# A fifth raw weight tile, the output projection's B21 split before its T4, and the context gate's tiles taken from the raw ring

## The chip, the core and the metric

The kernel runs as one program on one core of a Trainium2 chip. The metric is the device time of one execution in microseconds (us). Three runs of the kernel before took 925.86, 922.6 and 922.02 us, median 922.6.

## The reference, cut to what matters

One layer of a token mixer with a gated feed-forward network, on 512 tokens of width 1024 in float32, with 256 context tokens whose scan states start the scans of the main tokens. The parts that the change touches:

```python
la = jax.nn.log_sigmoid(lr @ w2 + b2) / 16      # gate of each head, for tokens and for context
o, s_f, s_b = _gla_bidir(q, k, v, lr, w2, b2, s0f, s0b)   # 4 heads, both directions, s0 from the context
...
merged = sigmoid(ga) * (a @ w_br_a) + sigmoid(gb) * (ob @ w_br_b)
x = x + g1 * (merged @ w_o)                     # the output projection
h2 = rms_norm(x) * (1 + scale) + shift
a, val = split(h2 @ w_up)                       # ffn, then a 3x3 convolution, gelu, and w_down
```

The last lines stand in a shortened form. The modulations (g1, scale, shift) are dot products of silu(c) with w_ada.

## The kernel before, in words

Every large product runs on TensorE with float32 operands taken apart into a high and a low half: the high half (wh, a cast) is made on ScalarE, the low half (wl, the weight minus its high half) on VectorE, and each product is three matmuls, high x high, high x low and low x high. So each weight tile costs ScalarE one 128x1024 cast (L149) and VectorE one 128x1024 subtraction (L150), both in `split_new`.

Weights arrive as raw tiles. They come from one ring, the tag `raw`, with four tiles; the load of a fifth weight waits until the first tile has been split. The high and low halves have rings of their own, with five tiles each. The list `specs` holds the splits in the order in which products use them, and `loads` what has to be loaded ahead of each; `weights` hands out the next split, makes the splits up to a lead (`stream_split`), and issues loads further ahead (`stream_load`). As every engine and the load queue on SyncE (SP) work strictly in program order, the place at which these calls stand in the code decides what waits behind what.

The square projections use a Strassen scheme of seven products on 512x512 blocks: `strassen` runs the products, `w_strassen` lists the weight splits. For the output projection (w_o, `low_first`) the products come in the order a11, s3, s2, s1, a22, a12, s4, each in two halves j. Their weights are B11, T3, T2, B12, T4, B21 and B22. T2 and T4 are sums of blocks, made in the tiles tt (L223 casts and L224 subtractions in `split_t`, sums at L236 and by accumulating loads of GpSimd). Between s2 and s1 the sum so far is copied from one pair of PSUM banks to another, on ScalarE (L483), and another sum is added into the first pair on VectorE (L484). `wo_done` takes each finished bank: `wo_gate` multiplies it with g1 (L1511, tile yt), `wo_add` adds it to the residual (L1515, tile x), `wo_sq` sums squares (L1518). The products of s4 end in the last pair of banks, for tokens 0 and 1 and the second half of the columns. Once these two yt are made, `low_norm` turns the second norm's outputs around for the ffn: transposes on TensorE (L1495), high and low halves h2h and h2l (L1503, L1504, L1506, L1507). The xs of the norm are scaled on ScalarE (L1487). The first ffn products are L402.

`wo_step` counts the 14 product halves; at the last of them it makes four more splits of ffn weights at once, so that these stand in the engines' queues ahead of the last yt.

The gate of the context tokens (`zc_head`, `zc_tail`, once per head) reads one PSUM bank (zc) into two tiles of the general ring `heap`: lc by ScalarE (L851), mc by VectorE (L853), then Exp, Ln, two scans on VectorE (L863), Exp (L865), and the product with the context's keys (L931), before TensorE transposes it (L949). `zx_head` and `zx_tail` do the same for the main tokens, with four short scans for each direction (L902). The rings also set order: a tile or a bank that is not yet free holds up what writes it.

In the opening, `cs` holds silu(c) for both modulations, in 32 columns for each of 8 blocks, cleared first (L527); the later modulations `ada2` read one column of it (L1190). `ones` is a constant 128x128 tile, and `ones_r` a rounded copy of it.

Of the kernel before, what the change touches and what calls it, by code (L numbers as in the profile page):

```python
# [8 lines left out]
F32 = mybir.dt.float32  # L9
F32R = mybir.dt.float32r  # L10
# [3 lines left out]
ALU = mybir.AluOpType  # L14
AX = mybir.AxisListType

P = 128
# [16 lines left out]
def backbone_kernel(  # L34
# [19 lines left out]
    def nm(s):  # L54
        cnt[0] += 1
        return f"{s}_{cnt[0]}"
# [16 lines left out]
    def const(shape, s, dt=F32):  # L73
        return cp.tile(shape, dt, tag=s, name=s)
# [23 lines left out]
    def table_for(func):  # L98
# [4 lines left out]

    ident = const([P, P], "ident")
    make_identity(nc, ident)
    ones = const([P, P], "ones")
    G.memset(ones, 1.0)
    maskf = const([P, P], "maskf")
    G.affine_select(out=maskf, in_=ones, pattern=[[1, P]], base=0, channel_multiplier=-1,
                    compare_op=ALU.is_ge, fill=0.0)  # L110
    maskb = const([P, P], "maskb")
    G.affine_select(out=maskb, in_=ones, pattern=[[-1, P]], base=0, channel_multiplier=1,
                    compare_op=ALU.is_ge, fill=0.0)
    eps_t = const([P, 1], "eps_t")
    G.memset(eps_t, EPS)
# [25 lines left out]
    specs, loads, last_load = [], [], {}  # L141

    def raw_tile(kn, n):
        return wp.tile([P, kn, n], F32, tag="raw", name=nm("raw"), bufs=4)

    def split_new(raw, kn, n):
        wh = wp.tile([P, kn, n], F32R, tag="wh", name=nm("wh"))
        wl = wp.tile([P, kn, n], F32R, tag="wl", name=nm("wl"))
        A.copy(wh, raw)  # L149
        V.tensor_tensor(wl, raw, wh.bitcast(F32), op=ALU.subtract)  # L150
        return wh, wl

    def w_cols(w, c0, n=P, k0=0, kn=KT, scaled=False):
        ap = w[k0 * P:(k0 + kn) * P, c0:c0 + n].rearrange("(k p) c -> p k c", p=P)
# [28 lines left out]
    def w_strassen(w, c0, add_b12=False, low_first=False):  # L183
# [58 lines left out]
        def split_b11(j):  # L242
            def split():
# [4 lines left out]
        js = range(2)  # L248
        b21, t1 = [split_raw("b21", j) for j in js], [split_raw("b12", j) for j in js]
        t4 = [lambda j=j: split_t(j) for j in js]  # L250
        specs.extend([split_b11(j) for j in js] + [(lambda j=j: split_t(j)) for j in js] + [split_t2(j) for j in js] +
                     (t1 + t4 + b21 if low_first else b21 + t1 + t4) + [split_raw("b22", j) for j in js])
        for o, fs in ((0, [load_raw("b11", 0, 0, j) for j in js]), (2, [load_t(j) for j in js]),
# [43 lines left out]
    def weights(lead=1, ahead=AHEAD):  # L297
# [9 lines left out]
    NG = len(GROUPS)  # L307
    G0 = [sum(GROUPS[:i]) for i in range(NG)]
    fv = [tuple(wp.tile([P, 2, 512], dt, tag=tag, name=nm(tag), **kw)
                for tag, dt, kw in (("raw", F32, dict(bufs=4)), ("wh", F32R, {}), ("wl", F32R, {})))  # L310
          for _ in range(4)]
    fqk = []
    w_lr = late([P, KT, 32], s="w_lr")
# [209 lines left out]
    A.activation(sg, cT, AF.Exp, scale=-1.0)  # L523
    V.tensor_scalar(sg, sg, 1.0, None, op0=ALU.add)
    V.reciprocal(sg, sg)
    cs = const([P, KT, 32], "cs")
    V.memset(cs, 0.0)  # L527
    V.tensor_tensor(cs[:, :, 0], cT[:, 0:8], sg[:, 0:8], op=ALU.mult)
    V.tensor_tensor(cs[:, :, 1], cT[:, 8:16], sg[:, 8:16], op=ALU.mult)

    selm = const([P, 4], "selm")
    for i in range(4):
# [308 lines left out]
    def zc_head(h):  # L841
        S_ = heads[h]
        bcol, wz = gate_col(h)
        zc = gl()
        for d in range(2):
            T.matmul(zc[:, d * LC:(d + 1) * LC], wz[d], lrc, start=True, stop=True)

        l = heap([P, 2, LC], s="lc")
        m = heap([P, 2, LC], s="mc")
        for d in range(2):  # L850
            A.activation(l[:, d, :], zc[:, d * LC:(d + 1) * LC], AF.Abs, bias=bcol[d])  # L851
        for d in range(2):
            V.tensor_scalar(m[:, d, :], zc[:, d * LC:(d + 1) * LC], bcol[d], 0.0, op0=ALU.add, op1=ALU.min)  # L853
        S_["zc"] = l, m
# [322 lines left out]
    def ada2(kinds):  # L1177
# [8 lines left out]
        for k in range(KT):  # L1186
            for a_, (_, _, c0) in zip(acc, todo_):
                w_ = late([P, 512], s="wa2")
                dma(w_, w_ada[0, k * P:(k + 1) * P, c0:c0 + 512])
                V.scalar_tensor_tensor(a_, w_, cs[:, k, 0:1], a_, op0=ALU.mult, op1=ALU.add)  # L1190
                yield
        parts = []
        for a_ in acc:
# [29 lines left out]
        V.tensor_copy(ccol[:, i * 110:(i + 1) * 110], ps[:, :110])  # L1223

    bg.extend([ada2(("g1", "sh")), ada2(("sc",))])
    ones_r = const([P, P], "ones_r", F32R)
    V.tensor_copy(ones_r, ones)


    a_act = []  # L1230

# [285 lines left out]
    def wo_sq(hf, t, tmp):  # L1517
        A.activation(tmp, x1[t][hf], AF.Square, accum_out=ss2[:, t, hf:hf + 1])  # L1518

    tmps = {}  # L1520

    def wo_done(hf, t, src, sign):
        if hf and t < 2:
            tmps[hf, t] = wo_gate(hf, t, src)
            if t == 1:
                low_norm()
            return
        tmp = wo_gate(hf, t, src)
        wo_add(hf, t, tmp, sign)
        if t < 2:  # L1530
            tmps[hf, t] = tmp
            return
        wo_sq(hf, t, tmp)
        if hf == 0:
            norm2_xs((t,), (norm2_root(t),))
            if t == 3:
                order_from.append(len(traced()))
# [20 lines left out]
    def wo_step():  # L1558
        count[0] += 1
        if count[0] == 1:  # L1560
            x1_load()
            table_for(AF.Sqrt)
        if count[0] == 14:
            stream_split(pos[2] + 4)
        do()

    strassen(lambda name, k, t: [z[:, k * P:(k + 1) * P] for z in mg[name, t]], wo_done, wo_step, True)
# [69 lines left out]
    def d_raw(kind, p):  # L1637
        if kind == "b22":
            t_ = heap([P, 512], s="b22")
            dma(t_, tokens(2 * p + 1)[:, 512:])  # L1640
            G.dma_start(t_, tokens(2 * p)[:, 512:], accum_op=ALU.add)  # L1641
        else:
            t_ = wp.tile([P, 2, 512], F32, tag="raw", name=nm("raw"), bufs=4)
            dma(t_, tokens(2 * p + (kind == "rb")).rearrange("p (a c) -> p a c", c=512))
        dq[kind, p] = t_

# [289 lines left out]
```

## Time and profile before

| | us |
|---|---|
| median of three runs | 922.6 |
| the profiled execution | 921.73 |
| its span, from the first to the last instruction | 919.7 |
| TensorE busy | 899.5 |
| VectorE busy | 755.4 |
| ScalarE busy | 484.7 |
| mean granted TensorE clock | 0.995 of full |

PE is TensorE, DVE VectorE, ACT ScalarE, POOL GpSimd and SP the engine that issues most loads. The span is cut into 40 slices of 23 us; in all but the first and the last of them, and one in the middle, TensorE is busy for 90% and more. Matmuls overlap: one counts as busy from its start to its end, although the next starts before that end, so short gaps don't show in the busy time. They show in the view of waits and in the starts of the single matmuls. In a row of the timeline stand the start, the duration, the engine, the line, the operation, the tile written and those read, the shapes and the count; in brackets stand the idle time before it and what ended it.

### The profile page before, as it was taken

The numbers are of one execution on the slowest core, as the hardware profiler recorded it, in microseconds if no ns is written. First come the engines' busy times: TensorE is split into PE (matmuls) and PEld (weight loads), VectorE is DVE, ScalarE is ACT, GpSimd is POOL, SyncE is SP. The second block draws the span as 40 slices with busy tenths as digits, with TensorE's granted clock in tenths as the row PEclk, the third lists the DMA queues.
The fourth block names the chain that finished last, engine by engine and source line by source line (L and its number), as shares of the span: only waits on it lengthen the run. The fifth ranks groups of instructions, "written<-read, shape, count | busy, mean of one in ns | idle before, by whom it ended". The sixth has DMA issues, their size and how long they took to land.

```text
span 919.7 us, 12868 instructions
## 1 busy us (share of the span) xinstructions
PE 899.5 (98%) x4671; PEld 756.4 (82%) x4671; DVE 755.4 (82%) x1307; ACT 484.7 (53%) x869; POOL 62.8 (7%) x98
## 2 busy tenths in 40 slices
PE   7999999999999999999999998999999999999996
PEld 5777899988888888888888888988888888888885
DVE  5667686779589877978776887899998888899896
ACT  5156464657466447566552568543333443356673
POOL 3000000000000011113011010000000000122100
PEclk9999999999999999999999999999999999999998
DMA  9950512142088375978578164264444333399532
GB/s 275 338 159 1 154 31 59 34 115 70 15 279 306 97 202 124 288 171 219 160 206 206 33 175 138 69 178 131 126 131 133 104 91 115 79 231 260 151 92 92
DMA packets 125821, 134.27 MB, mean 146 GB/s; under 512 B 7178, under 2 KB 84310, under 8 KB 125758
## 3 DMA queue, kind: packets, MB, share of 16 engines
q1 hardware_dynamic: 115357, 116.80, 41.0%
q0 software_dynamic: 8672, 15.43, 10.3%
q10 hardware_dynamic: 1728, 1.22, 0.4%
q8 instruction: 37, 0.61, 0.3%
q14 instruction: 27, 0.21, 0.1%
HBM read 131.32 MB, written 2.10 MB: 145 GB/s over the span
## 4 chain that ended last, share of the span: by engine, by line
PE 89%; DVE 6%; ACT 2%; issue 1%; DMA 1%; ACTq 0%; DVEq 0%
PE mm L387 31%; PE mm L418 11%; PE gl L465 7%; PE gl L1719 6%; PE mm L465 5%; PE mm L1719 4%; PE gl L418 4%; PE gl L935 3%; PE mm L402 3%; PE mm L708 2%; PE mm L411 2%; PE gl L708 1%; PE mm L1041 1%; DVE mx L902 1%; PE gl L631 1%
## 5 line engine op out<-in xcount | busy, mean ns | idle before, releaser
L149 ACT CAST wh<-raw 128x1024 fp32r<-128x1024 f32 x110 | 115.0, 1050 | 113.4 <-PE mm L387 73.1
L150 DVE TENSOR_TENSOR wl<-raw,wh 128x1024 fp32r<-128x1024 f32 x110 | 133.6, 1220 | 34.2 <-ACT wh L149 31.7
L1602 DVE SCALAR_TENSOR_TENSOR cacc<-ca,ccol,cacc 128x441 f32<-128x441 f32 (+2 forms) x176 | 121.0, 693 | 6.7 <-ACT cacc L1590 3.6
L387 PE MATMUL mm<-h2l,wh 128*128 128x512 f32 x320 | 124.5, 389 | 0.0
L387 PE MATMUL mm<-h2h,wl 128*128 128x512 f32 x320 | 124.5, 389 | 0.0
L387 PE MATMUL mm<-h2h,wh 128*128 128x512 f32 x320 | 124.5, 389 | 0.0
L387 PEld LDWEIGHTS mm<-h2h,wl 128*128 128x128 f32 x320 | 60.1, 188 | 12.6
L387 PEld LDWEIGHTS mm<-h2l,wh 128*128 128x128 f32 x320 | 60.1, 188 | 12.5
L387 PEld LDWEIGHTS mm<-h2h,wh 128*128 128x128 f32 x320 | 60.1, 188 | 12.4
L1190 DVE SCALAR_TENSOR_TENSOR acc<-wa,cs,acc 128x512 f32<-128x512 f32 x64 | 45.8, 747 | 3.4 <-DMA wa<-in_w_ada_dram 3.4
L1605 ACT ACTIVATE cacc<-cacc 128x512 f32<-128x512 f32 x22 | 13.9, 632 | 60.6 <-DVE cacc L1602 60.5
L387 PE MATMUL mm<-hxh,wh 128*128 128x512 f32 x104 | 41.7, 401 | 0.0
L387 PE MATMUL mm<-hxh,wl 128*128 128x512 f32 x104 | 40.9, 394 | 0.0
L387 PE MATMUL mm<-hxl,wh 128*128 128x512 f32 x104 | 40.5, 390 | 0.0
L223 ACT CAST wh<-tt 128x512 fp32r<-128x512 f32 x48 | 28.3, 621 | 20.4 <-DMA tt<-in_w_in_dram 7.5
L224 DVE TENSOR_TENSOR wl<-tt,wh 128x512 fp32r<-128x512 f32 x48 | 31.6, 687 | 7.9 <-ACT wh L223 7.8
L1661 ACT CAST wh<-raw 128x1024 fp32r<-128x1024 f32 x22 | 23.0, 1052 | 18.2 <-PE mm L1719 9.0
L199 POOL DMA_DIRECT2D tt<-in_w_in_dram x24 | 20.8, 1064 | 165.5 <-DVE xl L1291 71.8
L1662 DVE TENSOR_TENSOR wl<-raw,wh 128x1024 fp32r<-128x1024 f32 x22 | 26.9, 1223 | 2.6 <-ACT wh L1661 2.6
L1641 POOL DMA_DIRECT2D b<-in_ffn_w_down_dram x11 | 9.4, 865 | 276.8 <-DMA b<-in_ffn_w_down_dram 268.3
L465 PE MATMUL mm<-wh,hxh 128*128 128x512 f32 x72 | 28.0, 389 | 0.0
L465 PE MATMUL mm<-wl,hxh 128*128 128x512 f32 x72 | 28.0, 389 | 0.0
(527 smaller groups left out, 2449.9 us busy)
## 6 DMA issues: line engine op xcount, KB each, us to landing
raw<-in_w_in_dram SPq DMA_DIRECT2D x54, 512.0 KB, 4.6
wa<-in_w_ada_dram SPq DMA_DIRECT2D x96, 256.0 KB, 5.0
raw<-in_ffn_w_up_dram SPq DMA_DIRECT2D x44, 512.0 KB, 3.9
raw<-in_ffn_w_down_dram SPq DMA_DIRECT2D x22, 512.0 KB, 3.3
tt<-in_w_in_dram POOLq DMA_DIRECT2D x24, 256.0 KB, 6.5
raw<-in_w_br_a_dram SPq DMA_DIRECT2D x8, 512.0 KB, 5.2
raw<-in_w_br_b_dram SPq DMA_DIRECT2D x8, 512.0 KB, 3.8
raw<-in_w_o_dram SPq DMA_DIRECT2D x8, 512.0 KB, 6.0
```

The costliest lines, as they stand in the source:

```text
L149: A.copy(wh, raw)
L150: V.tensor_tensor(wl, raw, wh.bitcast(F32), op=ALU.subtract)
L223: A.copy(wh[:, kk, :], tt[j][kk])
L224: V.tensor_tensor(wl[:, kk, :], tt[j][kk], wh[:, kk, :].bitcast(F32), op=ALU.subtract)
L387: T.matmul(ps, a[:, k, :], b[:, c0:c0 + n], start=(k == 0 and i == 0), stop=(k == KT - 1 and i == 2))
L402: T.matmul(pss[u], a[:, k, :], b[:, c0:c0 + n], start=(k == 0 and z == 0), stop=(k == KT - 1 and z == 2))
L418: T.matmul(ps, a, b[:, k % 2, :], start=(k == 0 and i == 0), stop=(k == KT - 1 and i == 2))
L465: T.matmul(ps[t], a, b[:, kk, :], start=(first and i == 0), stop=(j == 1 and kk == 1 and i == 2), skip_group_check=again)
L708: T.matmul(fps[i], a, b, start=(k == 0 and z == 0), stop=(k == KT - 1 and z == 2))
L1190: V.scalar_tensor_tensor(a_, w_, cs[:, k, 0:1], a_, op0=ALU.mult, op1=ALU.add)
L1602: V.scalar_tensor_tensor(o, a_[:, r0 + dy:r1 + dy, c0 + dx:c1 + dx], wcol(tap), o, op0=ALU.mult, op1=ALU.add)
L1719: T.matmul(ps, a[:, t * P:(t + 1) * P], w[b][:, j, c0:c0 + n], start=(first and i == 0), stop=(last and i == 2), skip_group_check=again)
```

## The change

Five edits go together:

- The ring `raw` has five tiles instead of four.
- Room: `ones` is now `ones_r` read as plain float32, its first copy a short-lived tile; `cs` is a tile of `heap`, cleared where it is used, and its one column that is read later is kept in a small constant `c_col`.
- The context gate's two tiles lc and mc are the two halves of one raw tile, `lm`.
- In the output projection the split of half j of T4 is preceded by the load and the split of half j of B21; the products keep their order and take B21 from `kept`.
- At the last product half the low half of the fourth ffn weight is put off until the last two yt have been made.

```diff
-        return wp.tile([P, kn, n], F32, tag="raw", name=nm("raw"), bufs=4)
+        return wp.tile([P, kn, n], F32, tag="raw", name=nm("raw"), bufs=5)
...
         A.copy(wh, raw)
-        V.tensor_tensor(wl, raw, wh.bitcast(F32), op=ALU.subtract)
+        low = lambda: V.tensor_tensor(wl, raw, wh.bitcast(F32), op=ALU.subtract)
+        if low_later:
+            low_later[0].append(low)
+        else:
+            low()
         return wh, wl
...
         t4 = [lambda j=j: split_t(j) for j in js]
+        if low_first:
+            kept = {}
+
+            def split_both(j):
+                stream_load(base + 11 + j)
+                kept[j] = split_raw("b21", j)()
+                return split_t(j)
+
+            t4 = [lambda j=j: split_both(j) for j in js]
+            b21 = [lambda j=j: kept.pop(j) for j in js]
...
-    cs = const([P, KT, 32], "cs")
+    cs = heap([P, KT, 32], s="cs")
     V.memset(cs, 0.0)
...
+    c_col = const([P, KT], "c_col")
+    V.tensor_copy(c_col, cs[:, :, 0])
...
-        l = heap([P, 2, LC], s="lc")
-        m = heap([P, 2, LC], s="mc")
+        lm = wp.tile([P, 4, LC], F32, tag="raw", name=nm("lm"), bufs=5)
+        l, m = lm[:, 0:2, :], lm[:, 2:4, :]
...
             tmps[hf, t] = wo_gate(hf, t, src)
             if t == 1:
+                for low in later:
+                    low()
                 low_norm()
...
         if count[0] == 14:
+            low_later.append(later)
             stream_split(pos[2] + 4)
+            low_later.clear()
         do()
```

What this does to the engines' programs shows in three places. Line numbers differ between the two kernels: L149 and L150 become L152 and L153, L223 and L224 become L232 and L233, L483 is L502, L1511 is L1529, L853 is L874 and L902 is L923.

First, ScalarE in the middle of the output projection, ahead of the product s1. The casts wh<-raw of 128x1024 are weights from raw tiles, wh<-tt are halves of T4, gl<-gl are the copies between PSUM banks. Before:

```order
L149 CAST wh_5551<-raw_5449 128x1024
L223 CAST wh_5569<-tt_5174 128x512
L223 CAST wh_5569<-tt_5175 128x512
L483 COPY gl_5589<-gl_5503 128x512
L483 COPY gl_5590<-gl_5504 128x512
L223 CAST wh_5595<-tt_5434 128x512
L149 CAST wh_5615<-raw_5555 128x1024
L223 CAST wh_5595<-tt_5435 128x512
L149 CAST wh_5643<-raw_5575 128x1024
```

And after:

```order
L152 CAST wh_5549<-raw_5447 128x1024
L152 CAST wh_5567<-raw_5553 128x1024
L232 CAST wh_5571<-tt_5172 128x512
L232 CAST wh_5571<-tt_5173 128x512
L502 COPY gl_5591<-gl_5501 128x512
L502 COPY gl_5592<-gl_5502 128x512
L152 CAST wh_5597<-raw_5577 128x1024
L232 CAST wh_5601<-tt_5432 128x512
L232 CAST wh_5601<-tt_5433 128x512
L152 CAST wh_5659<-raw_5607 128x1024
```

The first half of B21 (raw_5553) is cast ahead of the first half of T4 and the two bank copies, and the second (raw_5577) behind the copies, where before both halves of B21 (raw_5555, raw_5575) stood between and behind the second half of T4.

Second, VectorE at the end of the output projection. Rows wl<-raw are low halves of weights, yt and x rows the gated sums and the residual. Before:

```order
L509 RECIPROCAL rstd_5685<-rstd_5685 128x1
L1477 TENSOR_REDUCE n2s_5696<-ss_5405 128x1
L1511 TENSOR_TENSOR yt_5741<-mm_5422,g_786_3789 128x512
L1515 TENSOR_TENSOR x_1135_5464<-x_1135_5464,yt_5741 128x512
L1511 TENSOR_TENSOR yt_5744<-mm_5423,g_786_3789 128x512
L509 RECIPROCAL rstd_5698<-rstd_5698 128x1
L1515 TENSOR_TENSOR x_1137_5468<-x_1137_5468,yt_5744 128x512
L150 TENSOR_TENSOR wl_5748<-raw_5665,wh_5747 128x1024
L150 TENSOR_TENSOR wl_5766<-raw_5709,wh_5765 128x1024
L150 TENSOR_TENSOR wl_5784<-raw_5727,wh_5783 128x1024
L1511 TENSOR_TENSOR yt_5787<-gl_5589,g_788_3794 128x512
L1511 TENSOR_TENSOR yt_5789<-gl_5590,g_788_3794 128x512
```

And after:

```order
L528 RECIPROCAL rstd_5683<-rstd_5683 128x1
L1495 TENSOR_REDUCE n2s_5694<-ss_5403 128x1
L1533 TENSOR_TENSOR x_1133_5462<-x_1133_5462,yt_5739 128x512
L1529 TENSOR_TENSOR yt_5742<-mm_5421,g_784_3787 128x512
L1533 TENSOR_TENSOR x_1135_5466<-x_1135_5466,yt_5742 128x512
L528 RECIPROCAL rstd_5696<-rstd_5696 128x1
L153 TENSOR_TENSOR wl_5746<-raw_5663,wh_5745 128x1024
L153 TENSOR_TENSOR wl_5764<-raw_5707,wh_5763 128x1024
L1529 TENSOR_TENSOR yt_5784<-gl_5591,g_786_3792 128x512
L1529 TENSOR_TENSOR yt_5786<-gl_5592,g_786_3792 128x512
L153 TENSOR_TENSOR wl_5782<-raw_5725,wh_5781 128x1024
```

Ahead of the last two yt (from the banks gl) stand two low halves instead of three, and the third comes behind them. Further up in the same queue, between the last half of T4 (wl<-tt) and these rows, the two low halves of B21 are gone: they stand ahead of the halves of T4.

Third, VectorE in head 1 of the scans, around the context gate (mc before, lm now; mx are the gates of the main tokens, vx their values, o the outputs of the head before). Before:

```order
L928 TENSOR_TENSOR mx_1454<-kq_1167,mx_1454 128x512
L927 TENSOR_TENSOR lx_1452<-kq_921,lx_1452 128x512
L1019 COPY o_1097<-gl_1560 128x256
L853 TENSOR_SCALAR mc_1460<-gl_1456,vec_b 128x256 x2
L1019 COPY o_1098<-gl_1573 128x256
L730 TENSOR_TENSOR vx_1402<-mm_1586,vx_1401 128x256
L863 SCALAR_TENSOR_TENSOR mc_1460<-mc_1460,lc_1459 128x256 x2
L1019 COPY o_1097<-gl_1613 128x256
```

And after:

```order
L999 TENSOR_TENSOR st_1306<-stt_1395,st_1305 128x256
L874 TENSOR_SCALAR lm_1462<-gl_1459,vec_b 128x256 x2
L906 TENSOR_SCALAR mx_1457<-gl_1449,vec_b 128x512
L923 SCALAR_TENSOR_TENSOR mx_1453<-mx_1453,lx_1451 128x128 x4
L927 TENSOR_TENSOR dec_1475<-mx_1453 128x4
L934 TENSOR_TENSOR lx_1451<-mx_1453 128x512
L929 TENSOR_TENSOR dec_1475<-dec_1475,mx_1453 128x3
L930 COPY dec_1475<-mx_1453 128x1
L923 SCALAR_TENSOR_TENSOR mx_1457<-mx_1457,lx_1455 128x128 x4
L884 SCALAR_TENSOR_TENSOR lm_1462<-lm_1462 128x256
```

The read of the context gate's bank (mc or lm from gl) stood behind the four products with the keys (L927, L928) and an output copy; now it stands ahead of the scans of the main tokens. Its own scans (L884, before L863) follow those. In head 2 it moves in the same way. In head 0 the gate's scans and the product behind them go ahead of the first low halves of the weights that the other heads' context uses.

More of the change, by code (lines that the diff above doesn't have):

```diff
@@ L105, in backbone_kernel @@
     make_identity(nc, ident)
-    ones = const([P, P], "ones")
-    G.memset(ones, 1.0)
+    ones_w = late([P, P], s="ones")
+    G.memset(ones_w, 1.0)
+    ones_r = const([P, P], "ones_r", F32R)
+    V.tensor_copy(ones_r, ones_w)
+    ones = ones_r.bitcast(F32)
     maskf = const([P, P], "maskf")
-    G.affine_select(out=maskf, in_=ones, pattern=[[1, P]], base=0, channel_multiplier=-1,
+    G.affine_select(out=maskf, in_=ones_w, pattern=[[1, P]], base=0, channel_multiplier=-1,
                     compare_op=ALU.is_ge, fill=0.0)
     maskb = const([P, P], "maskb")
-    G.affine_select(out=maskb, in_=ones, pattern=[[-1, P]], base=0, channel_multiplier=1,
+    G.affine_select(out=maskb, in_=ones_w, pattern=[[-1, P]], base=0, channel_multiplier=1,
                     compare_op=ALU.is_ge, fill=0.0)
@@ L149, in split_new @@
         A.copy(wh, raw)
-        V.tensor_tensor(wl, raw, wh.bitcast(F32), op=ALU.subtract)
+        low = lambda: V.tensor_tensor(wl, raw, wh.bitcast(F32), op=ALU.subtract)
[3 more added lines that the diff above has]
+            low()
         return wh, wl
+    low_later = []
     def w_cols(w, c0, n=P, k0=0, kn=KT, scaled=False):
@@ L309, in backbone_kernel @@
     fv = [tuple(wp.tile([P, 2, 512], dt, tag=tag, name=nm(tag), **kw)
-                for tag, dt, kw in (("raw", F32, dict(bufs=4)), ("wh", F32R, {}), ("wl", F32R, {})))
+                for tag, dt, kw in (("raw", F32, dict(bufs=5)), ("wh", F32R, {}), ("wl", F32R, {})))
           for _ in range(4)]
@@ L1189, in ada2 @@
                 dma(w_, w_ada[0, k * P:(k + 1) * P, c0:c0 + 512])
-                V.scalar_tensor_tensor(a_, w_, cs[:, k, 0:1], a_, op0=ALU.mult, op1=ALU.add)
+                V.scalar_tensor_tensor(a_, w_, c_col[:, k:k + 1], a_, op0=ALU.mult, op1=ALU.add)
                 yield
@@ L1225, in backbone_kernel @@
     bg.extend([ada2(("g1", "sh")), ada2(("sc",))])
-    ones_r = const([P, P], "ones_r", F32R)
-    V.tensor_copy(ones_r, ones)
     a_act = []
@@ L1518, in wo_sq @@
         A.activation(tmp, x1[t][hf], AF.Square, accum_out=ss2[:, t, hf:hf + 1])
-    tmps = {}
+    tmps, later = {}, []
     def wo_done(hf, t, src, sign):
@@ L1642, in d_raw @@
         else:
-            t_ = wp.tile([P, 2, 512], F32, tag="raw", name=nm("raw"), bufs=4)
+            t_ = wp.tile([P, 2, 512], F32, tag="raw", name=nm("raw"), bufs=5)
             dma(t_, tokens(2 * p + (kind == "rb")).rearrange("p (a c) -> p a c", c=512))
```

## The prediction

> **What bounds the kernel now.** I read the page first, then the view of what each engine waited for, then the timeline around each place where TensorE waited. The page's chain by engine, and the longest of the eight rows of TensorE's waits with the one that will matter:
>
> ```profile
> PE 89%; DVE 6%; ACT 2%; issue 1%; DMA 1%; ACTq 0%; DVEq 0%
> PE mm L515 <- DMA rows<-in_b_ada_dram: 5.8, 1, 5.8
> PE gl L1495 <- DVE yt L1511: 2.6, 1, 2.6
> PE gl L935 <- DVE mc L853: 1.2, 2, 0.7
> PE gl L465 <- ACT gl L483: 0.2, 1, 0.2
> ```
>
> In a row of waits stand who waited for what, then us in total, times and the longest. TensorE is the bound: it holds 89% of the chain and waits little. The change keeps every matmul, so it can win only what TensorE waits for. It leaves the longest wait (the first rows from memory) alone and touches three rows: yt (the end of the output projection), mc (the context gate), and L483 (the middle of the output projection). The four rows not shown are of 0.6 us and less, in the opening and head 0.
>
> A wait costs more than its idle time if the clock falls. The timeline of TensorE at the end of the output projection (start, duration, line, tiles, count, and in brackets the idle time before), and behind it the row of a stretch with busy times by engine and, third from the end, the granted clock, 1.00 being full:
>
> ```profile
> 555.59 0.40 PE L465 MATMUL gl<-wh,ml 128*128 128x512 f32 x1
> 555.82 1.23 PE L1495 MATMUL gl<-ident,xs 128*128 128x128 f32 x8
> 559.66 1.97 PE L1495 MATMUL gl<-ident,xs 128*128 128x128 f32 x8 [2.61 <-DVE yt L1511]
> 561.28 1.20 PE L402 MATMUL mm<-h2h,wh 128*128 128x256 f32 x4
> 562.28 0.78 PE L402 MATMUL mm<-h2h,wl 128*128 128x256 f32 x4
> 562.90 0.64 PE L402 MATMUL mm<-h2l,wh 128*128 128x256 f32 x4
> 563.37 0.28 PE L402 MATMUL mm<-h2h,wh 128*128 128x256 f32 x1
> 563.49 0.28 PE L402 MATMUL mm<-h2h,wl 128*128 128x256 f32 x1
> ```
>
> ```profile
> 559.10:562.60 3.50, 2.94 (x14) 2.94 (x15) 3.47 (x8) 3.50 (x10) 0.00 (x0) 0.51 1.05 305
> ```
>
> After 2.61 us of idling the clock is 0.51 for 3.5 us. Eight transposes take 1.97 us where the eight before took 1.23 (+0.74). Four L402 matmuls take 1.00 us from start to start and the next four 0.62, where the single ones step by 0.12, that is 0.48 for four (+0.52, +0.14). Slow work: 1.4 us. The gap itself is 2.61, or 2.77 from start to start, since transposes overlap by some 0.16. The yt wait is worth 4.2 us.
>
> **The end of the output projection.** Why is yt late? VectorE, from the last half of T4 on (the first three and the last two rows of an unbroken queue):
>
> ```profile
> 540.39 0.69 DVE L224 TENSOR_TENSOR wl<-tt,wh 128x512 fp32r<-128x512 f32 x1 [2.19 <-ACT wh L223]
> 541.00 1.22 DVE L150 TENSOR_TENSOR wl<-raw,wh 128x1024 fp32r<-128x1024 f32 x1
> 542.13 0.68 DVE L495 TENSOR_TENSOR es<-gl,es 128x512 f32<-128x512 f32 x1
> ...
> 555.51 3.49 DVE L150 TENSOR_TENSOR wl<-raw,wh 128x1024 fp32r<-128x1024 f32 x3
> 558.92 1.28 DVE L1511 TENSOR_TENSOR yt<-gl,g 128x512 f32<-128x512 f32 x2
> ```
>
> No row from 541.00 to 558.92 shows idle time, so the yt pair comes as late as the queue ahead is long. In it stand eight low halves of weights (L150): B21 twice, B22 twice, four of the ffn. With the change both of B21 go ahead of 540.39, and the fourth of the ffn goes behind yt: five are left. Each is 1.13 (541.00 to 542.13), so yt moves 3 x 1.13 = 3.4 forward, to 555.5. The second yt also needs the last sum, which ends at 555.59 + 0.40 = 556.0. TensorE has done its first eight transposes at 557.05 (555.82 + 1.23). What shifts the sums shifts the transposes too, and behind the second yt's 0.64 (half of the pair's 1.28) TensorE still has four transposes that need the first yt alone. So the wait goes whole, and with it the slow clock: -2.77 - 1.41.
>
> The price is paid at the other end, on ScalarE. B21's high half goes into a run of casts that TensorE already waits for:
>
> ```profile
> 531.06 1.05 ACT L149 CAST wh<-raw 128x1024 fp32r<-128x1024 f32 x1
> 532.01 1.14 ACT L223 CAST wh<-tt 128x512 fp32r<-128x512 f32 x2
> 533.30 1.06 ACT L483 COPY gl<-gl 128x512 f32<-128x512 f32 x2
> 533.33 0.39 PE L465 MATMUL gl<-wh,ml 128*128 128x512 f32 x1
> 533.92 0.50 PE L465 MATMUL gl<-wh,mh 128*128 128x512 f32 x1 [0.21 <-ACT gl L483]
> ```
>
> The copies L483 come directly behind the casts, and s1's first matmul (533.92) behind the first copy. One more cast is 0.95 (531.06 to 532.01), so s1 starts 0.95 later: +0.95. The gap grows from 0.59 start to start (0.23 is the normal step) to 1.54. Behind the second B21 cast stand only T4's second halves, for which VectorE waits 2.19 as it is (540.39 above), so that one is covered; cover gone, it would be another 0.95. Below, the cost is 0 if ScalarE had room that the rows don't show; above, it is 0.95 and a fall of the clock (1.4): none follows the 0.85 us gap of head 1 below (granted clock 1.00 in its stretch), one follows 2.61, and 1.3 over the step lies nearer the first. I take 0.95.
>
> What is late next? High parts and xs of norm 2, on ScalarE:
>
> ```profile
> 557.47 0.56 ACT L1503 ACTIVATE h2h<-gl,col_sh,am 128x256 fp32r<-128x256 f32 x1
> 566.65 2.55 ACT L1487 ACTIVATE xs<-x,rstd 128x512 f32<-128x512 f32 x4
> 572.02 0.60 PE L1495 MATMUL gl<-ident,xs 128*128 128x128 f32 x4
> ```
>
> ScalarE's work between the first two rows starts when the first transposes are done, now at about 557.4 instead of 557.47, so it gains nothing; TensorE does. Its transposes at 572.02 move to 572.02 - 3.23 = 568.8 and need the first two xs, ready at 566.65 + 1.3 = 568.0. That holds by 0.8. So -4.18 + 0.95 = -3.2 here.
>
> [...]
>
> **The context gate.** Its two tiles came from the heap ring and come from the raw ring now, so heads 1 and 2 read the gate's PSUM bank ahead of the long scans. TensorE waits for that bank once in each (the second pair of rows is head 2; the third row is the stretch around head 1, its granted clock third from the end):
>
> ```profile
> 134.09 0.28 PE L411 MATMUL mm<-wh,hcl 128*128 128x256 f32 x1
> 135.06 0.50 PE L935 MATMUL gl<-st,qh 128*128 128x256 f32 x2 [0.69 <-DVE mc L853]
> 115.00:138.00 23.00, 22.31 (x179) 21.79 (x178) 20.19 (x54) 15.25 (x37) 0.20 (x2) 1.00 0.10 31
> 174.39 0.28 PE L935 MATMUL gl<-vx,ptl 128*128 128x256 f32 x1
> 175.13 0.51 PE L935 MATMUL gl<-st,qh 128*128 128x256 f32 x2 [0.47 <-DVE mc L853]
> ```
>
> From start to start 0.97 and 0.74 where 0.12 is the step, as above: 0.85 + 0.62 = 1.47, -1.5. Nothing is added on VectorE: the gate's steps go ahead, and evictions of values go behind. What comes next there are the gate's transposes, which no row of the waits names now. Below, the gain is 0 if they become late by as much; above it can't exceed the two gaps.
>
> Head 0 pays a little. VectorE and ScalarE split the first two ctx weights between the gate's steps; now the steps go first:
>
> ```profile
> 88.57 0.65 ACT L859 ACTIVATE lc<-lc 128x512 f32<-128x512 f32 x1
> 90.40 1.22 DVE L150 TENSOR_TENSOR wl<-raw,wh 128x1024 fp32r<-128x1024 f32 x1
> 91.53 1.27 DVE L863 TENSOR_TENSOR_SCAN mc<-mc,lc 128x256 f32<-128x256 f32 x2
> 93.12 0.39 PE L387 MATMUL mm<-hxh,wl 128*128 128x512 f32 x1
> ```
>
> ScalarE's Exp ends at 89.2 and Ln, as long, at 89.8; two scans are 1.27; an Exp of half the width follows, 0.3 by the first row; then one cast, 0.95, and one low half, 1.22. That is 93.5, where TensorE wants it at 93.12. +0.3 (0 if the steps overlap by more than that; at most the 1.2 of one low half).
>
> **The rest at nothing.** The fifth raw tile brings loads forward, but no row of TensorE's waits names a weight's load. In the opening, the clearing of cs (128x256) and a copy of 128x8 go behind the reciprocal, in front of a stretch where VectorE idles 0.47 for ScalarE:
>
> ```profile
> 7.93 0.16 DVE L550 TENSOR_TENSOR ss<-ss 128x1 f32<-128x1 f32 x1 [0.47 <-ACT junk L546]
> ```
>
> The two together, by the 0.68 of a 128x512 operation above, are about 0.35 to 0.7; without that cover this is what they would cost. Reordered low halves in the ffn and its down projection never pass their first reader, so they cost 0 as long as the queue of VectorE runs ahead of TensorE there, as it does now.
>
> **Sum**, from the profiled execution (921.73 us, 2.0 of it around the span): -2.77 - 1.41 + 0.95 - 1.47 + 0.3 = -4.4, that is 917.3. The median of the runs, 922.6, is 0.9 above the profiled one; with it, 918.2.
>
> **Rivals.** First, a wait takes the place of yt, or s1's gap trips the clock. One more low half ahead of yt, or ScalarE later with xs by the 0.8 of cover and more, is 1.1; the clock at s1 is 1.4. For it speaks the thin cover, against it that yt at 555.5 is 1.5 ahead of 557.05. It gives 919.4.
>
> Second, the gate's time is given back in the same heads, because scans and evictions that were pushed back hold up the transposes: 1.5 less won, 919.7. Against it: nothing waits for them now. With the first rival as well it is 921.
>
> Third, ScalarE has room at s1, and the 0.95 isn't paid: 917.2. Against it: the three ScalarE rows there leave no gap.
>
> Fourth, the slow 1.4 us don't hang on the gap, because the clock falls there in any case: 919.6. The 0.51 that begins at the gap's end speaks against it. [...]
>
> Fifth, and slower: B21's cast waits for its load, and all of ScalarE's casts behind it. The loads of this weight (count, size, median us from issue to landing), and what their queue waits for:
>
> ```profile
> raw<-in_w_o_dram SPq DMA_DIRECT2D x8, 512.0 KB, 6.0
> SPq L193 <- DVE tt L236: 76.5, 8, 28.5
> ```
>
> These loads wait for T2's sums (L236) to free a tile, up to 28.5 us, and take 6.0. With a fifth tile the first B21 can go early and lands long before 532.0. The rival decides from an issue at 526.0 on, microsecond for microsecond; 4.4 later the gain is eaten. Issued only at 532.0, it would land at 538.0, s1 would start 6.0 later, the clock would fall (1.4), and 922.6 - 4.4 + 6.0 + 1.4 gives 925.6.
>
> **How the numbers follow.** Forecast 0.45; first rival 0.22; second 0.11, both 0.07; third 0.07; fourth 0.02; fifth 0.06. The range leaves out the fifth and the far ends of the others: below, 921.7 - 5.65 = 916.1 (everything won, nothing paid, no shift to the median), less 0.3 for scatter; above, the first two rivals together, 921.0, and 0.6, the distance of the two closer runs before. About 0.5% (4.6 us) is what a measurement of this kernel can tell from no change. It is reached at 918.0, just below my forecast: somewhat over half of the forecast's chance, taken with the scatter, lies on the side of no change, with the first, second and fourth rivals: 0.57. The rest and the third give faster 0.36; the fifth, rounded up, slower 0.07.
>
> **What would show it.** In the changed kernel's profile: no wait of the transposes for yt above 0.3, and a granted clock of 1.00 there; the wait for the L483 copy at 1.1 to 1.2 instead of 0.2; no row for the gate's tile; a wait of 0.3 or less for a low half in head 0. I am wrong if the list of waits names a DMA, xs or a raw tile, or if the clock falls after s1.

## The result, and the profile after

| us | before | after |
|---|---|---|
| median (of 6 runs each) | 923.26 | 916.86 |
| lowest and highest run | 922.02, 925.86 | 916.64, 917.57 |
| profiled execution | 921.73 | 916.85 |
| its span | 919.7 | 914.9 |

The changed kernel takes 0.9931 of the time before, with a 95% interval of 0.9919 to 0.9944: faster by 0.7%. From profile to profile the gain is 4.9, between the medians it is 6.4, and the runs of the changed kernel lie much closer together; over all its runs on record the kernel before took between 920.1 and 926.3. So two things need an explanation, the gain and the scatter that went.

What TensorE waited for in the changed kernel (us in total, times, longest), the first two of seven rows and the one of head 0:

```profile
PE mm L534 <- DMA rows<-in_b_ada_dram: 5.9, 1, 5.9
PE mm L484 <- DVE wl L153: 0.6, 1, 0.6
...
PE mm L406 <- DVE wl L153: 0.3, 1, 0.3
```

The rows for yt, for the gate's tile and for the L483 copy are gone. New are two waits for low halves of weights. The end of the output projection, first TensorE, then VectorE, then the row of the whole stretch (granted clock third from the end):

```profile
555.00 0.39 PE L484 MATMUL gl<-wh,ml 128*128 128x512 f32 x1
555.23 1.91 PE L1513 MATMUL gl<-ident,xs 128*128 128x128 f32 x16
556.89 0.72 PE L421 MATMUL mm<-h2h,wh 128*128 128x256 f32 x4
```

```profile
552.53 2.34 DVE L153 TENSOR_TENSOR wl<-raw,wh 128x1024 fp32r<-128x1024 f32 x2
554.79 1.33 DVE L1529 TENSOR_TENSOR yt<-gl,g 128x512 f32<-128x512 f32 x2
556.03 1.22 DVE L153 TENSOR_TENSOR wl<-raw,wh 128x1024 fp32r<-128x1024 f32 x1
```

```profile
552.00:575.00 23.00, 23.00 (x182) 22.23 (x182) 17.06 (x41) 19.39 (x41) 0.00 (x0) 1.00 0.36 103
```

The sixteen transposes now stand in one row, the ffn's products come at once, and the clock stays at 1.00. The yt pair starts at 554.79 behind two low halves, and the third follows it.

The middle of the output projection, TensorE ahead of s1, and the rows of ScalarE and VectorE that it depends on:

```profile
532.34 0.39 PE L484 MATMUL gl<-wh,ml 128*128 128x512 f32 x1
532.56 0.39 PE L484 MATMUL mm<-wh,mh 128*128 128x512 f32 x1
533.56 0.50 PE L484 MATMUL mm<-wl,mh 128*128 128x512 f32 x1 [0.61 <-DVE wl L153]
533.90 0.40 PE L484 MATMUL gl<-wh,mh 128*128 128x512 f32 x1
```

```profile
530.06 2.00 ACT L152 CAST wh<-raw 128x1024 fp32r<-128x1024 f32 x2
531.97 1.14 ACT L232 CAST wh<-tt 128x512 fp32r<-128x512 f32 x2
533.00 1.05 ACT L502 COPY gl<-gl 128x512 f32<-128x512 f32 x2
```

```profile
531.15 2.36 DVE L153 TENSOR_TENSOR wl<-raw,wh 128x1024 fp32r<-128x1024 f32 x2
```

Two products that write a bank mm now stand ahead of s1, which writes gl. They belong to a12, the product with B21; as B21 is split so early, its first two matmuls could be placed there. The second of them waits for B21's low half (the second of the two in the VectorE row), and s1 follows directly; the copy that s1 needs, which started at 533.00, is no longer what TensorE waits for.

The starts of the same matmuls in the two profiles, subtracted, give the change by place:

| place | forecast | measured |
|---|---|---|
| opening | 0 | +0.44 |
| head 0 | +0.3 | +0.66 |
| heads 1 and 2 | -1.47 | -1.61 |
| head 3, and up to the output projection | 0 | -0.47 |
| s1, with the two matmuls moved ahead of it | +0.95 | +0.39 |
| yt wait and slow clock | -4.18 | -4.23 |
| sum | -4.4 | -4.8 |

The opening differs from execution to execution: at 25 us, the profiles of the changed kernel and of its variants below lie between 0.1 ahead of the kernel before and 1.0 behind it. So its +0.44 can't be put down to the change.

### The profile page after: what moved, and what is told of

It reads as the page before. It is cut to its first block, busy times and chain, and to the rows that moved or that the text cites. A ratio compares the mean times of both kernels' runs of the same rounds, so it can differ in the third digit from the quotient of the medians.

```text
span 914.9 us, 12857 instructions
## 1 busy us (share of the span) xinstructions
PE 897.5 (98%) x4671; PEld 755.7 (83%) x4671; DVE 755.6 (83%) x1308; ACT 485.0 (53%) x869; POOL 62.8 (7%) x98
## 4 chain that ended last, share of the span: by engine, by line
PE 96%; DVE 2%; ACT 1%; DMA 0%; issue 0%; ACTq 0%
PE mm L406 32%; PE mm L437 11%; PE gl L484 9%; PE mm L484 7%; PE gl L1741 6%; PE mm L1741 4%; PE mm L430 4%; PE gl L437 4%; PE gl L956 3%; PE mm L421 3%; PE mm L729 2%; PE gl L729 1%; PE gl L652 1%; PE gl L989 1%; PE gl L1253 1%; PE mm L629 1%
## 5 line engine op out<-in xcount | busy, mean ns | idle before, releaser
L152 ACT CAST wh<-raw 128x1024 fp32r<-128x1024 f32 x110 | 114.7, 1049 | 102.5 <-PE mm L406 71.0
L153 DVE TENSOR_TENSOR wl<-raw,wh 128x1024 fp32r<-128x1024 f32 x110 | 133.4, 1219 | 27.0 <-ACT wh L152 21.8
L406 PE MATMUL mm<-h2h,wh 128*128 128x512 f32 x320 | 124.5, 389 | 0.0
L406 PE MATMUL mm<-h2l,wh 128*128 128x512 f32 x320 | 124.5, 389 | 0.0
L406 PE MATMUL mm<-h2h,wl 128*128 128x512 f32 x320 | 124.5, 389 | 0.0
L406 PEld LDWEIGHTS mm<-h2h,wl 128*128 128x128 f32 x320 | 60.1, 188 | 12.6
L406 PEld LDWEIGHTS mm<-h2l,wh 128*128 128x128 f32 x320 | 60.1, 188 | 12.5
L406 PEld LDWEIGHTS mm<-h2h,wh 128*128 128x128 f32 x320 | 60.1, 188 | 12.3
L1211 DVE SCALAR_TENSOR_TENSOR acc<-wa,c_col,acc 128x512 f32<-128x512 f32 x64 | 45.6, 745 | 4.0 <-DMA wa<-in_w_ada_dram 4.0
L406 PE MATMUL mm<-hxh,wh 128*128 128x512 f32 x104 | 41.7, 401 | 0.0
L406 PE MATMUL mm<-hxh,wl 128*128 128x512 f32 x104 | 41.1, 395 | 0.3 <-DVE wl L153 0.3
L406 PE MATMUL mm<-hxl,wh 128*128 128x512 f32 x104 | 40.6, 390 | 0.0
L232 ACT CAST wh<-tt 128x512 fp32r<-128x512 f32 x48 | 28.4, 619 | 17.9 <-PE mm L484 4.4
L233 DVE TENSOR_TENSOR wl<-tt,wh 128x512 fp32r<-128x512 f32 x48 | 31.6, 685 | 6.7 <-ACT wh L232 6.7
L484 PE MATMUL mm<-wh,hxl 128*128 128x512 f32 x72 | 28.0, 389 | 0.0
```

The lines of the kernel that those rows point to most:

```text
L153: low = lambda: V.tensor_tensor(wl, raw, wh.bitcast(F32), op=ALU.subtract)
L232: A.copy(wh[:, kk, :], tt[j][kk])
L233: V.tensor_tensor(wl[:, kk, :], tt[j][kk], wh[:, kk, :].bitcast(F32), op=ALU.subtract)
L406: T.matmul(ps, a[:, k, :], b[:, c0:c0 + n], start=(k == 0 and i == 0), stop=(k == KT - 1 and i == 2))
L484: T.matmul(ps[t], a, b[:, kk, :], start=(first and i == 0), stop=(j == 1 and kk == 1 and i == 2), skip_group_check=again)
L1211: V.scalar_tensor_tensor(a_, w_, c_col[:, k:k + 1], a_, op0=ALU.mult, op1=ALU.add)
```

## The experiments: the parts of the change

Each of the first four kernels is the changed one with one part undone. Line numbers shift by a few lines with each edit.

**B21 in its old place.** The block that splits B21 ahead of T4 is left out.

```diff
-        if low_first:
-            kept = {}
-            def split_both(j):
...
-            b21 = [lambda j=j: kept.pop(j) for j in js]
```

> The changed kernel with B21 split in its old place, behind T4; all else stays. Theory (the yt wait is VectorE's queue, the price at s1 is ScalarE's): seven low halves of weights instead of five stand between T4 and the yt pair, so the transposes wait for yt again, about 1.5 us idle instead of 0 (before: 2.61 with eight), and s1's step shrinks by about 0.4. If the clock stays at 1.00 after this gap: 916.9 - 0.4 + 1.6 = 918.1. If a gap of 1.5 us is enough for the clock to fall, 1.4 more: 919.5. Rival (B21's place matters neither to yt nor to s1): 916.9, no wait for yt.

Measured: 918.23 (917.79 to 919.1). The rows of its profile that matter:

```profile
555.15 1.03 PE L1503 MATMUL gl<-ident,xs 128*128 128x128 f32 x8
556.87 1.25 PE L1503 MATMUL gl<-ident,xs 128*128 128x128 f32 x8 [0.69 <-DVE yt L1519]
```

```profile
PE gl L474 <- ACT gl L492: 0.2, 1, 0.2
```

The wait for yt is back, s1 waits 0.2 for the copy as before, and the two matmuls of a12 are back behind a22. Against the changed kernel's profile s1 wins 0.40. But the wait for yt is 0.7, not 1.5: T4's second half was ready earlier than before the change (the last of its low halves on VectorE at 538.74 instead of 540.39, TensorE being only 0.7 earlier), as the fifth tile stays in this kernel; the kernel with the fifth tile alone, below, bears this out (539.67, with TensorE at the same time as before). So the place of B21 is worth 1.4 of the change's gain, and the rest of the old wait came from the postponed low half and from loads.

**The low half not postponed.**

```diff
-            low_later.append(later)
             stream_split(pos[2] + 4)
-            low_later.clear()
```

> The changed kernel without the postponed low halves: one more low half of the ffn's weights (1.13 us) stands ahead of the yt pair, nothing else moves. Theory: yt starts at 554.8 + 1.1 = 555.9 instead of 554.8, its first half is done 0.7 later, where the ninth transpose wants it at 556.1: a wait of 0.3 to 0.4 and about 0.6 to 0.7 us longer, 917.5; clock 1.00. Rival (there is more cover than that, and the postponement does nothing): 916.9, no row for yt.

Measured: 917.7 (917.26 to 918.65), a wait for yt of 0.7, clock 1.00 there. The price is near the one expected (0.84 between the medians, 0.88 in the steps); the wait itself is 0.3 longer than worked out, because the third low half had to wait for its high half:

```profile
554.54 1.23 DVE L153 TENSOR_TENSOR wl<-raw,wh 128x1024 fp32r<-128x1024 f32 x1 [0.40 <-ACT wh L152]
555.68 1.28 DVE L1529 TENSOR_TENSOR yt<-gl,g 128x512 f32<-128x512 f32 x2
```

As this execution is 0.5 ahead of the changed kernel's profile up to here, the yt pair starts 1.4 later and not 1.1, and TensorE loses 0.9 of it. In the changed kernel the yt pair comes just in time.

**The gate's tiles in the heap.**

```diff
-        lm = wp.tile([P, 4, LC], F32, tag="raw", name=nm("lm"), bufs=5)
-        l, m = lm[:, 0:2, :], lm[:, 2:4, :]
+        l = heap([P, 2, LC], s="lc")
+        m = heap([P, 2, LC], s="mc")
```

> The changed kernel with the context gate's two tiles back in the heap ring. Theory: the waits for the gate's tile return in heads 1 and 2 (0.9 + 0.7 by the steps of the matmuls in the two traces) and head 0 loses its 0.7: 916.9 + 1.6 - 0.7 = 917.8, up to 918.1 if the 0.3 gained in head 3 comes from the gate's tiles too. Rival (the time gained in heads 1 and 2 is given back elsewhere): within 0.3 of 916.9.

Measured: 918.01 (917.58 to 918.6). The wait for the gate's tile is back as it was, and the one for a low half in head 0 (L406) is gone:

```profile
PE gl L956 <- DVE mc L874: 1.2, 2, 0.7
```

So the gate's part is worth 1.15 net. In the steps, heads 1 and 2 lose 0.94 and 0.72, and head 3 loses 0.33: most of the -0.47 that the table has behind head 2 hangs on the gate's tiles too.

**Head 0's gate in the heap, the others in the raw ring.** The three lines above, under `if h:` for the raw tile and `else:` for the heap.

> The changed kernel with head 0's gate tiles in the heap ring, those of heads 1 to 3 in the raw ring. Theory (head 0's price is the two low halves of the ctx weights behind the gate's steps): the wait for a low half in head 0 goes, 0.7 us less, 916.2. Rival (head 0's later matmuls are a shift that began in the opening, and heads 1 and 2 depend on head 0's order): 916.9 or more.

Measured: 915.68 (915.49 to 916.84), and, measured again later, 916.74 beside 917.33 for the changed kernel. In the steps head 0 wins 0.7 both times; the other 0.5 of the first time lay ahead of 25 us, in the opening. The heads behind are not touched.

## The experiments: where the spread came from

**The kernel before, profiled once more.**

> The kernel before, unchanged, profiled once more: its runs spread over 5.8 us (920.1 to 925.9) where the changed kernel's spread over 0.9. Theory (the yt wait makes the spread: its size and the fall of the clock differ from execution to execution): where the time of this execution differs from the 921.7 of the first profile, the difference lies at the yt wait, within 0.5 us of it, and TensorE's steps up to 533 lie as before. Rival (the spread comes from the opening or from loads elsewhere): the yt wait is 2.6 again and the difference lies elsewhere.

Measured: 922.17, span 920.2, and neither theory. Up to 380 us every matmul starts 0.33 later than in the first profile of before; at 412 it is 1.75 later; behind the yt wait 0.47. So this execution lost 1.4 at a place where the first one lost nothing, and then did not pay for the clock. First, the place. ScalarE and TensorE in the gating products (second weight), this execution:

```profile
407.16 1.05 ACT L149 CAST wh<-raw 128x1024 fp32r<-128x1024 f32 x1 [4.35 <-DMA raw<-in_w_in_dram]
409.52 0.50 PE L465 MATMUL mm<-wl,hxh 128*128 128x512 f32 x1 [0.51 <-DVE wl L150]
```

and the same cast in the first profile of before, behind which TensorE waited for nothing:

```profile
405.41 1.05 ACT L149 CAST wh<-raw 128x1024 fp32r<-128x1024 f32 x1 [3.51 <-DMA raw<-in_w_in_dram]
```

The cast waits for its load in both. In the first execution the load came just in time for TensorE, in the second 0.85 later relative to its issue. The load had been issued at 398.82 and 399.72, only 6.6 and 7.4 ahead of the cast, as the ring had no free tile earlier:

```profile
398.82 0.37 SPq L193 DMA_DIRECT2D raw<-in_w_in_dram  x1
399.72 0.37 SPq L193 DMA_DIRECT2D raw<-in_w_in_dram  x1
```

Second, the clock. The wait for yt was 2.6 again, yet no slow stretch followed. In the first profile the record of the granted clock begins at 9.607 with 1.00 (the opening's 128x256 matmuls of L608 take 634 ns ahead of this and 379 ns behind it). At 559.153, after 549.546, it falls to 0.50 for 3.413; then it is 1.00 for 351.573, and at 914.139 it falls for the rest of the span. The three lengths are 161.0, 1 and 103.0 times 3.413. In the changed kernel the record begins at 10.612 and falls first at 908.318, 263.0 times 3.413 behind its beginning; in this execution it begins at 9.985. Cut into steps of 3.413, counted from the beginning of the record (in each row the length of the stretch, then TensorE's busy time), the first profile of before and then this one:

```profile
555.74:559.15 3.41, 1.31 (x10) 0.75 (x7) 3.41 (x4) 3.41 (x7) 0.00 (x0) 1.00 0.57 167
559.15:562.57 3.42, 2.91 (x14) 2.91 (x15) 3.39 (x8) 3.42 (x10) 0.00 (x0) 0.50 1.05 304
```

```profile
556.12:559.53 3.41, 2.59 (x15) 1.86 (x14) 3.41 (x6) 3.41 (x5) 0.00 (x0) 1.00 0.65 187
559.53:562.95 3.42, 1.64 (x13) 1.47 (x14) 3.42 (x6) 3.42 (x10) 0.00 (x0) 1.00 0.98 279
562.95:566.36 3.41, 3.41 (x31) 3.41 (x30) 2.97 (x9) 3.41 (x10) 0.00 (x0) 1.00 0.68 180
```

In the first the gap fell mostly into one step (2.1 idle), and the next step ran at half clock. In the second it lay across two (0.8 and 1.8 idle), and the clock stayed at 1.00 in both and in the step behind them.

**A gap of 3 us on purpose.** The postponed low half goes back ahead of yt and is made three times.

```diff
             low_later.clear()
+            for low in 3 * later:
+                low()
+            later.clear()
```

> The changed kernel with three extra low halves ahead of the last yt pair: the postponed one and two repetitions of it (the same values are written again). With one the transposes waited 0.7 us; with three 0.7 + 2 x 1.13 = 3.0, somewhat more than before's 2.61. Without a fall of the clock: 917.7 + 2.3 = 920.0. With the fall in every execution: 921.4 to 921.7. Theory (the fall depends on where the gap lies to the throttle's own grid of 3.41 us, which begins at another time in every execution): runs of both kinds, a spread of over 1.4 us, and in the profile a clock record that begins a whole number of 3.41 us after the first. Rival (the gap trips the clock always or never): a spread below 1 us as in the changed kernel.

Measured: 921.57, twelve runs from 920.08 to 923.22, with mean clocks from 0.992 to 0.997. The wait is 3.0, and the profiled execution shows a fall one step long:

```profile
556.44:559.85 3.41, 0.56 (x4) 0.42 (x4) 3.38 (x5) 3.41 (x10) 0.00 (x0) 1.00 0.57 162
559.85:563.26 3.41, 3.41 (x17) 3.38 (x17) 3.34 (x9) 3.41 (x10) 0.00 (x0) 0.50 0.53 152
```

The spread is 3.1 over twelve runs; the twelve runs of the changed kernel (two sets of six) lie within 1.3, and the three low halves ahead of yt are the only difference. So a gap of this size scatters the runs, as the theory has it. The clock explains only a part: the two runs at 0.997 took 920.1 and 920.3, the ones at 0.992 and 0.994 took 922.7 and 922.6, but the slowest, 923.2, had a mean of 0.996.

**Four raw tiles in the changed kernel.** `bufs=4` in place of `bufs=5`.

> The changed kernel with four raw tiles instead of five, the gate's tiles still among them. TensorE's order stays, that of VectorE and ScalarE changes a little outside the output projection. Theory (the fifth tile only brings loads forward that nothing waited for; B21's second load now lands at about 534.7, 0.7 after its cast was issued, with cover behind it): 916.9 to 917.6, no wait of TensorE for a load. Rival (the fifth in the prediction: B21's casts wait for their loads): s1 or the T4 products wait 2 us and more, 919 and above.

Measured: 919.46, twelve runs from 917.68 to 920.76, mean clocks from 0.996 to 0.998. Both theories fall: the output projection has no new wait, so the rival's place is wrong, but the fifth tile is far from worth nothing. The waits of TensorE and ScalarE that matter, in the profile of the slowest of the runs:

```profile
PE mm L484 <- DVE wl L153: 1.3, 2, 0.7
PE gl L484 <- ACT gl L493: 0.9, 1, 0.9
PE gl L484 <- DVE es L514: 0.6, 1, 0.6
```

```profile
ACT wh L152 <- DMA raw<-in_w_in_dram: 16.3, 6, 4.5
```

All but one of these waits of TensorE (B21's 0.6 at s1) lie between 380 and 412, in the gating products, and 3.4 are lost there against the changed kernel's profile. Another 0.8 is lost ahead of them, where TensorE waits 0.5 at 229 for values (vr) from ScalarE. ScalarE's row, for the changed kernel and for the first profile of before:

```profile
ACT wh L152 <- DMA raw<-in_w_in_dram: 3.3, 1, 3.3
```

```profile
ACT wh L149 <- DMA raw<-in_w_in_dram: 9.5, 4, 3.5
```

With five tiles ScalarE waited once for a raw tile of w_in, with four tiles four times in the kernel before and six times here. With five tiles the same loads are issued earlier, and ScalarE's casts run ahead. In the changed kernel, the loads on their queue (at 388.61 and 394.15, where the kernel before issued the two at 394.07 and 398.82), then the casts at the place of the waits above:

```profile
388.61 5.91 SPq L202 DMA_DIRECT2D raw<-in_w_in_dram  x2
```

```profile
400.40 1.06 ACT L152 CAST wh<-raw 128x1024 fp32r<-128x1024 f32 x1
401.69 1.05 ACT L152 CAST wh<-raw 128x1024 fp32r<-128x1024 f32 x1 [0.23 <-PE gl L484]
```

**The fifth tile alone.** The changed kernel with the gate in the heap, B21 in its old place and no postponed low half: the three edits shown above, together.

> The kernel before with the fifth raw tile and nothing else that orders the work: gate's tiles in the heap, B21 and the low halves in their old places. Theory (the fifth tile brings forward the loads of the second gating weight, whose casts came late by chance, TensorE waiting at 385 to 410 in some executions and not in others): that wait goes, and by adding the parts measured so far to the changed kernel, 916.9 + 1.15 (gate) + 1.4 (B21) + 1.1 (one more low half ahead of yt) = 920.5, 3 less than before, with runs closer together than before's 6 us; a wait for yt of about 1.8; no cast of a raw weight behind a DMA at 400 to 410. Rival (four tiles were only short because the gate's tiles had come into their ring): 922.5 and more, spread as before.

Measured: 922.01, twelve runs from 919.5 to 924.17; 0.9984 of before, 0.9972 to 0.9997. So alone the fifth tile is worth 1.3 (922.01 against 923.33), 1.5 less than the theory's sum has it. Its mechanism holds in the trace: TensorE is busy for all of 380 to 412, and no cast of a raw weight waits for a load there. What the sum left out is the clock. The wait for yt is still 2.1, and the runs are ordered by their mean granted clock:

| mean granted clock | runs | span, us |
|---|---|---|
| 0.997, 0.998 | 3 | 917.8, 919.1, 919.1 |
| 0.994 to 0.996 | 7 | 919.8 to 920.9 |
| 0.992 | 2 | 921.8, 922.5 |

A mean below 1 doesn't tell of a fall by itself: the end of the span, with no matmul in it, is at half clock too, for 5.6 us in the first profile of before (from 914.14), 6.6 in that of the changed kernel (from 908.32) and 7.3 in that of head 0's gate in the heap (from 906.37), and the last two of these, without another fall, have means of 0.996. But at 0.992 some 7 us of full clock are missing, where such an end (3.7 in the longest of the three) and one slow step (1.7) account for 5.4. By this estimate the two slowest runs had two slow steps or more; they have no trace.

The profile is that of the fastest, and there the step with most of the gap was 1.7 idle and not followed by a fall:

```profile
555.10:558.52 3.42, 1.74 (x12) 1.31 (x10) 3.42 (x4) 3.42 (x7) 0.00 (x0) 1.00 0.61 173
558.52:561.93 3.41, 2.98 (x24) 2.80 (x25) 3.38 (x8) 3.41 (x10) 0.00 (x0) 1.00 0.96 278
```

The spread as a whole, 4.7, is no smaller than that of the kernel before beside it (4.6, 17 runs), against the theory. But its make-up is another. At a mean clock of 0.994 or 0.995 the spans of this kernel lie between 919.8 and 920.9 (6 runs), those of the kernel before between 920.1 and 923.9 (11 runs): what the clock doesn't order goes with the fifth tile.

So the kernel before had two sources of scatter, the late loads and the gap with its clock, and the change takes both away: with loads that come late and no gap (four tiles in the changed kernel) the spread is 3.1, with a gap and no late loads (the fifth tile alone) it is 4.7, and without both it is 1.3, each over twelve runs.

## The experiments: a mended version

Two costs of the change could go: head 0's 0.7, by its gate tiles in the heap as above, and s1's 0.4, by splitting both halves of B21 just ahead of T4's second half.

```diff
             def split_both(j):
-                stream_load(base + 11 + j)
-                kept[j] = split_raw("b21", j)()
+                stream_load(base + 12)
+                if j:
+                    kept.update({i: split_raw("b21", i)() for i in js})
                 return split_t(j)
```

> The changed kernel with two edits: head 0's gate tiles in the heap ring, and both B21 splits just ahead of T4's second half, so that they stand behind the L483 copies on ScalarE. Theory: s1 gets its copies at the old time, and the 0.4 lost there come back, the cover (ScalarE idle for 1.8 and 1.3 us ahead of T4's second halves) takes both casts: 915.7 - 0.4 = 915.3, no wait for yt. Rival (both casts of 0.95 push T4's casts, VectorE's queue and yt back): a wait for yt of 0.5 to 1 us, 916 and above.

Measured: 916.07 (915.69 to 916.51), above the 915.68 of head 0 alone, which was measured at another time. The steps show s1 as expected, and no wait for yt:

```profile
531.74 1.06 ACT L503 COPY gl<-gl 128x512 f32<-128x512 f32 x2 [0.15 <-PE gl L485]
532.70 2.01 ACT L152 CAST wh<-raw 128x1024 fp32r<-128x1024 f32 x2
535.42 0.62 ACT L232 CAST wh<-tt 128x512 fp32r<-128x512 f32 x1 [0.70 <-PE gl L485]
```

Both casts stand behind the copies and end ahead of T4's, which still wait. Against the profile of head 0 alone, 0.4 are won at s1, and 0.7 more are lost in the opening, ahead of 16 us. To see beyond this, the changed kernel and both mended ones ran once more beside each other.

> The changed kernel itself, beside the next two, to tell differences of some tenths: 916.9 again, runs within 1 us of each other.

> Head 0's gate tiles in the heap ring, once more. By the steps of the traces 0.6 less than the changed kernel: 916.3; the 1.2 less of the first time had 0.5 from the opening, whose slow stretch ends at another time in every execution.

> Head 0's gate tiles in the heap ring and B21's splits behind the L483 copies, once more. By the steps 0.6 + 0.4 = 1.0 less than the changed kernel: 915.9, and 0.4 less than the kernel with head 0 alone. Rival (the second edit gives its 0.4 back where no trace of one execution shows it): equal to that kernel or above it, as in the first look.

Measured: 917.33 (916.84 to 917.93), 916.74 (916.22 to 917.06) and 915.62 (915.12 to 916.52). The version with both edits is the fastest, 1.7 less than the changed kernel beside it, and every run of it lies below every run of that one; it takes 0.9913 of the time before (0.9898 to 0.9929). By the steps the edits are worth 0.7 and 0.4; what the medians show beyond this is of the size of the opening's scatter.

## Why the prediction was right, and where it was wrong

The direction and the range held, and the time was 1.3 below the forecast: 0.45 of it in the sum, 0.9 in the step from the profile to the median. That the sum came so near is in part luck: by the table its terms are off by +0.44 and +0.36 (opening, head 0) and by -0.47 and -0.56 (head 3 and behind it, s1), and these cancel for the most part. And the prediction gave 0.57 to no change, within 0.5%, and only 0.36 to faster; the measured 0.7%, with its interval from 0.56% to 0.81%, lies beyond that mark.

**The yt wait** was read rightly, in mechanism and size: VectorE's queue ahead of yt, the two B21 low halves and the postponed one out of it, -4.23 against -4.18. The two kernels that undo its parts (918.23, 917.7) wait for yt again. That the cover is thin was right too.

**The clock** was right for the profiled execution, since the slow 1.4 did hang on the gap, and the fourth rival falls: without the gap no profile of the changed kernel or of the mended ones has a fall between the opening and the end (1.00 from 10.612 to 908.318 in the changed kernel; the mean clocks of the others are 0.996 and 0.997). But it is not a fixed price, as the prediction had it. The same wait of 2.6 was followed by it in one execution (0.50 for 3.41 us) and not in another (1.00), where the stretch from the wait on was 1.3 shorter. That the profile which the sum started from had the fall was chance.

**s1** is the step that was mis-sized: +0.95 in the sum, +0.39 measured. s1's first matmul did start 0.95 later relative to the work before it, but not by the path that was forecast: two matmuls of a12 stood ahead of it, and the second waited 0.61 for B21's low half on VectorE. That both come to 0.95 is luck. As the two matmuls are missing at their old place, 0.46 of it came back there. ScalarE was late as forecast, but its copies started 0.3 ahead of the forecast; half of this had stood in the prediction's own rows, where ScalarE is free at 533.15 and copies from 533.30 on, which the prediction read as no gap. The sign looked for (a wait of 1.1 to 1.2 for the copy) did not appear. The prediction looked at ScalarE's order there and not at TensorE's. With both B21 splits behind the copies, the 0.4 came back.

**The gate** was right in heads 1 and 2 (-1.61 against -1.47). Nothing was given back: undoing it costs 1.15. Head 0 was the right mechanism, two low halves that come later, at twice the size, +0.66 for +0.3.

**"The rest at nothing"** failed. It said that the fifth raw tile brings loads forward, but that no row of TensorE's waits names a weight's load. That was so in the one profile of before, because the late loads were covered there with nothing to spare. ScalarE's row showed them even then (9.5 us of waits for raw tiles of w_in). In the changed kernel, where the gate's tiles use the same ring, going back to four tiles costs 2.1 to 2.6, against its medians of 917.33 and 916.86; in the kernel before, a fifth tile alone wins 1.3. And the step that added 0.9 to go from the profile to the median took the scatter for a property of the measurement. It belonged for the most part to two places of the kernel, and the change removes both: after it, the profiled execution and the median differ by 0.01, and by 0.15 when measured again.

What stays open: how much of the scatter of before each of the two places makes, since only two of its executions have a trace; why the slowest run with the gap of 3 us took 923.2 at a mean clock that leaves room for one slow step; what the differences in the opening come from; and what the fall of the clock depends on. In mid-kernel, steps with 1.7 and 1.8 us idle were not followed by it, and steps with 2.1 and 2.85 were; but at the kernel's end a step with 1.6 idle, behind the last matmul, was (head 0's gate in the heap):

```profile
902.95:906.37 3.42, 1.78 (x14) 1.64 (x12) 2.99 (x9) 1.84 (x5) 0.00 (x0) 1.00 0.00 0
906.37:909.78 3.41, 0.00 (x0) 0.00 (x0) 2.56 (x8) 2.38 (x8) 0.00 (x0) 0.50 0.53 196
```

So in these profiles the idle time of one step doesn't decide it alone.

## What to carry to other kernels

An engine that feeds the bound one and itself waits for loads is a cost waiting to happen, even where the bound engine shows no wait: ask how much later the load could have come, and read a spread of runs far wider than scatter as a sign of such places. Price a gap of TensorE as its length plus a chance of the clock's fall (1.4 us here), and take away the gap rather than shorten it. Work that is moved early also frees what depends on it to move, so look at the order of the engine that uses it as well.

## What the runs showed of the hardware that was not expected

In the first profile of before and in that of the changed kernel, every change of the granted clock lay a whole number of times 3.413 us behind the beginning of its record (161, 162 and 265 times in the one, 263 times in the other), and the record began at another time in each execution (9.607 and 10.612; 9.985 in the second profile of before). A step of this length with TensorE idle for 2.1 us (first profile of before) or 2.85 us (the gap of 3 us) was followed by one step at 0.50; steps with 1.8 idle (second profile of before) and 1.7 idle (the fifth tile alone) in mid-kernel were not, and a step with 1.6 idle at the kernel's end was (head 0's gate in the heap). So the same kernel with the same wait of 2.6 ran with and without the slow step.
